# A transformer layer on one core: weight sums and norms in the passage into the feed-forward, and a rebuilt first stage

## The chip and the metric

The kernel runs on one core of a Trainium2 chip. Its engines are TensorE (PE, with its weight loads listed apart as PEld), VectorE (DVE), ScalarE (ACT), GpSimd (POOL), and SyncE (SP), which here issues nearly all DMAs. The metric is device time in microseconds (us). Of several runs the median is taken.

## What is computed

One layer over 1024 latent and 256 context tokens, model width 1024, all in f32:

```python
h = _modulate(_rmsnorm(x), sh_a, sc_a)          # for latent and context tokens
qa, ka, va, cq, ckv, krope = jnp.split(h @ w_in, SPLIT_POINTS, axis=-1)
# cq, ckv: own rmsnorm, then w_q_up, w_kv_up
oa = _map_query_blocks(lambda q1, q2: _diff_attend(q1, q2, k1, k2, va, lam), lq1, lq2)
ob = _map_query_blocks(lambda q: _softmax_attend(q, kb, vb), lqb)
new_lat = x_lat + g_a * _merge_heads(oa, ob, lam_init, diff_subln, w_out)
h = _modulate(_rmsnorm(new_lat), sh_f, sc_f)
new_lat = new_lat + g_f * _swiglu(h, w_ffn_in, w_ffn_out)
return _rmsnorm(new_lat, final_norm)
```

The shifts, scales and gates come from `silu(c) @ w_ada + b_ada`. `_rmsnorm` divides by the root of the mean square over the width.

## The kernel before

Activations lie transposed: 128 features on the partitions, tokens along the free axis, so that the width is eight chunks `k`. A product of full precision is made of a high and a low part (both fp32r): weights wh, wl and activations hH, hL, three products each. `split` makes the parts: ScalarE rounds to the high part, VectorE (or another engine, `lo_eng`) subtracts to get the low one.

The norm of a column of tokens needs a sum over partitions. `column_sums` multiplies tiles of 128 tokens with two columns of ones; `inverse_rms` takes root and reciprocal, and the result has tokens on the partitions. `spread` brings it back along the free axis: it scales the identity by each 128 of the values, which gives diagonals (`dg`), and multiplies them with ones on PE. `low_diag` and `low_norm` do so for the two low-rank inputs, `Attention.diagonal` and `Attention.spread` for the eight blocks of the differential heads, `stat` and `spread_stat` around the feed-forward and for the last norm.

In the first stage (`p1`, up to `st.close()`, line 604) the squares of x are added up, the norm is spread into `rstd`, and for each chunk `k` the modulation's shift and scale are computed (`load_ada`, `split_ada`, `ada_part`, `ada_row`, `ada_columns`), x is modulated into hH and hL (`modulate`), and `group` adds the chunk's part of seven products with the low-rank columns of w_in (`mixw`, `lows`). The modulation's weights are the moving operand, 256 columns of two halves at once, with four columns of c (`c4`) as the weights in PE. On PE, DVE, ACT and POOL the order of this stage is the order of the program; a DMA is issued when its tile comes free. The later products with w_in, w_q_up and w_kv_up follow, and PE's order is there written out with `run_tasks`.

Attention's order is made by a planner (`attention_graph`, `schedule`): each operation has an engine, an assumed length, dependencies and a priority. The output projection (`project`, `residual`) follows.

The feed-forward goes through hidden chunks of 128 in a scheme of seven products instead of eight. `Hidden.sums` forms sums of weight blocks, `odd` and `even` split them, `last` splits one block, `p1` to `p7` are the products, 12 matmuls each. The first two chunks are done in the passage (`with tc.manual_schedule(engines=ENGINES)`, line 1544), where the program's order holds on all four engines, beside the norm of the second 512 tokens (`stat(512, 512, ...)`), its scaling (`scale2`, `shift2`) and the differences and splits of the tokens (`part`, `run`, `t3`, `t4`). The remaining chunks are a plain loop. Then w_ffn_out's products and the last norm (`final`) follow.

## Time and profile before

| | |
|---|---|
| three runs | 1570.89, 1575.68, 1576.01 us, median 1575.68 |
| profiled execution | 1571.2 us, span 1569.3, mean granted clock 0.985 |
| PE busy | 1499.1 us, 96% of the span |
| DVE, ACT, POOL busy | 1123.8, 752.5, 787.0 us |
| chain that ended last | PE 70%, DVE 10%, DMA 6%, POOL 5% |

A profile row of a matmul gives the instruction, not the call: an f32 product is two of them, an fp32r product one. Times that stand beside each other on PE overlap, since matmuls are pipelined; from start to start is what one costs. Idle time of an engine stands in square brackets with what ended it. The granted clock is the share of full speed that the throttle gave TensorE: 1.00 is 2.4 GHz, 0.50 is 1.2 GHz.

### The profile page before, as it was taken

The page shows a single profiled execution, that of the slowest core. Times are in us where ns is not written, and L with a number is a line of the kernel's source. Part 1 is how long each engine was busy: PE and PEld are TensorE (multiplying, and loading weights), DVE is VectorE, ACT ScalarE, POOL GpSimd, SP SyncE. Part 2 cuts the span into 40 slices and gives each one's busy share as a digit, 9 for nine tenths or more (in the row PEclk, how much of TensorE's full clock was granted, in tenths as well). Part 3 has the DMA queues.
Part 4 walks back from the last instruction along what each step waited for, and adds up shares of the span by engine and source line. Part 5 has one row for each costly group of instructions (what it writes and reads, how often), then busy time and mean ns, then how long its engine had stood idle before and what let it go on. Part 6 is the DMA issues. An engine that isn't in the chain of part 4 may idle for free.

```text
span 1569.3 us, 20682 instructions
## 1 busy us (share of the span) xinstructions
PE 1499.1 (96%) x7323; PEld 1210.4 (77%) x7323; DVE 1123.8 (72%) x1630; ACT 752.5 (48%) x1184; POOL 787.0 (50%) x547
## 2 busy tenths in 40 slices
PE   4899999989999999999999989999999999999997
PEld 2577888866777878888878767888888888888876
DVE  5758565569999879999854697655555555899883
ACT  5443321157777766777753454333333333444451
POOL 2437245526777847756511565755544441484221
PEclk8899999999999999999999989999999999999999
DMA  8426988596344434533146302322222224975633
GB/s 262 140 80 215 318 293 241 179 272 164 91 104 110 121 108 128 121 115 98 58 117 186 128 27 81 121 81 81 81 81 81 81 81 136 358 271 180 208 101 108
DMA packets 153922, 227.69 MB, mean 145 GB/s; under 512 B 11215, under 2 KB 80859, under 8 KB 153819
## 3 DMA queue, kind: packets, MB, share of 16 engines
q1 hardware_dynamic: 153547, 226.11, 46.7%
q8 instruction: 58, 0.95, 0.2%
q14 instruction: 45, 0.37, 0.1%
q10 hardware_dynamic: 272, 0.26, 0.0%
HBM read 172.53 MB, written 53.81 MB: 144 GB/s over the span
## 4 chain that ended last, share of the span: by engine, by line
PE 70%; DVE 10%; DMA 6%; POOL 5%; issue 3%; ACT 3%; SPq 1%; DVEq 0%; ACTq 0%; POOLq 0%
PE mm L1427 25%; PE mm L1715 10%; PE S L1056 10%; PE T L1118 6%; PE acc L1135 4%; PE acc L1140 3%; PE mm L1355 3%; PE mm L410 2%; PE ps L1355 1%; DMA wa<-in_w_ada_dram 1%; PE mm L600 1%; POOL sh L645 1%; POOL macc L681 1%; PE S L1355 1%; POOL e L1104 1%
## 5 line engine op out<-in xcount | busy, mean ns | idle before, releaser
L1056 PE MATMUL S<-kt,qt 128*128 128x512 f32 (+1 forms) x768 | 197.9, 362 | 10.5 <-ACT e L1090 8.7
L1090 ACT ACTIVATE e<-S,nm 128x1280 f32<-128x1280 f32 x128 | 170.3, 1331 | 46.4 <-DVE nm L1076 37.9
L1715 PE MATMUL mm<-block 128*128 128x512 f32 x792 | 179.7, 389 | 0.0
L1122 ACT ACTIVATE ph<-T 128x512 fp32r<-128x512 f32 x240 | 140.3, 597 | 81.9 <-PE T L1118 77.7
L1715 PEld LDWEIGHTS mm<-block 128*128 128x128 f32 x792 | 148.7, 188 | 30.8
L1072 DVE TENSOR_REDUCE nm<-S 128x1 f32<-128x1024 f32 x128 | 156.2, 1220 | 22.5 <-PE S L1056 21.1
L1126 DVE TENSOR_TENSOR pl<-T,ph 128x512 fp32r<-128x512 f32 x240 | 160.0, 682 | 15.8 <-ACT ph L1122 15.0
L1056 PEld LDWEIGHTS S<-kt,qt 128*128 128x128 f32 x768 | 131.8, 189 | 39.1 <-ACT e L1090 15.1
L1118 PE MATMUL T<-ident,e 128*128 128x128 f32 x960 | 140.4, 274 | 3.1 <-DVE pl L1126 1.7
L1110 POOL TENSOR_SCALAR e<-e,ls 128x1280 f32<-128x1280 f32 x64 | 88.0, 1376 | 102.6 <-DVE ls L1107 71.5
L1118 PEld LDWEIGHTS T<-ident,e 128*128 128x128 f32 x960 | 114.0, 141 | 32.1 <-DVE pl L1126 6.4
L1135 PE MATMUL acc<-ph,vt 128*128 128x512 f32 x320 | 120.9, 418 | 1.1 <-DVE otmp L1156 1.0
L1427 PE MATMUL mm<-fresh,wh 128*128 128x512 f32 x352 | 114.8, 406 | 3.4 <-DVE fresh L1580 3.3
L1427 PE MATMUL mm<-block,wh 128*128 128x512 f32 x352 | 112.2, 400 | 0.0
L1140 PE MATMUL acc<-pl,vt 128*128 128x512 f32 x240 | 104.6, 436 | 0.0
L1532 POOL TENSOR_TENSOR hd<-acc,v 128x512 f32<-128x512 f32 x22 | 29.7, 1349 | 149.4 <-DVE acc L1528 137.8
L344 ACT ACTIVATE wh<-wf 128x1024 fp32r<-128x1024 f32 (+1 forms) x51 | 52.2, 1025 | 103.4 <-issue 68.2
L1300 POOL TENSOR_TENSOR acc<-acc,sq 128x512 f32<-128x512 f32 x23 | 34.3, 1489 | 124.6 <-ACT sq L1298 124.0
L1104 POOL TENSOR_TENSOR e<-e,e 128x1280 f32<-128x1280 f32 x32 | 94.2, 2944 | 2.7
L410 PE MATMUL mm<-hH,wh 128*128 128x512 f32 (+1 forms) x256 | 95.2, 372 | 0.0
L410 PE MATMUL mm<-hH,wl 128*128 128x512 f32 (+1 forms) x256 | 94.0, 367 | 0.0
L410 PE MATMUL mm<-hL,wh 128*128 128x512 f32 (+1 forms) x256 | 93.8, 367 | 0.0
(357 smaller groups left out, 3613.3 us busy)
## 6 DMA issues: line engine op xcount, KB each, us to landing
wf<-in_w_ffn_in_dram SPq DMA_DIRECT2D x44, 512.0 KB, 3.7
hidD<-hd SPq DMA_DIRECT2D x44, 256.0 KB, 2.1
wh<-in_w_ffn_out_dram SPq DMA_DIRECT2D x21, 512.0 KB, 5.3
wl<-hidD SPq DMA_DIRECT2D x17, 512.0 KB, 5.7
wa<-in_w_ada_dram SPq DMA_DIRECT2D x16, 512.0 KB, 4.0
wa<-in_w_ada_dram SPq DMA_DIRECT2D x32, 256.0 KB, 3.7
qt<-QB SPq DMA_DIRECT2D x32, 256.0 KB, 4.7
qt<-QA SPq DMA_DIRECT2D x32, 256.0 KB, 4.9
```

What stands on the lines that cost most here:

```text
L410: PE.matmul(ps, a(k), b(k), start=start and i == 0, stop=stop and i == n - 1)
L1056: m = PE.matmul(S[:, c0:c0 + w], q, k[:, k0:k0 + w], start=s == 0, stop=s == len(job) - 1)
L1072: on_banks(DVE.tensor_reduce(self.stats(n)[0][:, i:i + 1], sl, AX.X, ALU.max, negate=True), BANKS[i], DVE)
L1090: m = ACT.activation(e, S[:, i * NT:(i + 1) * NT], AF.Exp, bias=self.s[n][0][:, i:i + 1], accum_out=total)
L1104: POOL.tensor_tensor(self.e[n, 0], self.e[n, 0], self.e[n, 1], ALU.add)
L1118: PE.transpose(self.T[c][:, b * P:(b + 1) * P], e[:, kc * P:(kc + 1) * P], ident)
L1122: ACT.activation(self.ph[c], self.T[c], AF.Copy)
L1126: DVE.tensor_tensor(self.pl[c], self.T[c], f32(self.ph[c]), ALU.subtract)
L1135: PE.matmul(self.acc[u, qh, j], vt[:, kc, v], self.ph[c], start=kc == 0 and i == 0, stop=False)
L1140: PE.matmul(self.acc[u, qh, j], self.kv[u][1][:, kc, v], self.pl[c], start=False, stop=kc == 9)
L1427: PE.matmul(ps, a[:, k, :], b, start=k == 0 and i == 0, stop=k == 3 and i == 2)
L1715: PE.matmul(ps[d], w[:, sl], x[:, t0:t0 + n], start=first and c == 0 and i == 0, stop=c == NH - 1 and i == 2, skip_group_check=not first)
```

## The change

It has five parts.

1. `spread` has no diagonals any more: the 128 values are the weights of an f32 product, repeated over 128 columns, and the identity is the moving operand; one product for each 128 tokens. All norms use it, and attention's planner loses the eight `diagonal` steps.
2. The host lays w_in and w_out out by chunks of 128 columns, and the modulation's first 2048 columns by chunk (`w_first`), so that a load is one run of 4 KB for each partition.
3. In the first stage the loads of x alternate with those of weights. Chunks 0 to 2 of the modulation use the f32 weights unsplit (`ada_whole`), chunk 0 before the norm's sums, chunk 1 behind its spread, chunk 2 in the loop's first pass. Chunks 3 to 7 are split two passes ahead, both subtractions on DVE, into a tile for each half, so that `ada_parts` has 32 products of 128 columns where `ada_part` had 16 of 256. The column turn (`ada_turn`) ends a pass.
4. In the passage, both first chunks' weight sums go to DVE; the first chunk's subtractions too; the second chunk's `even` goes to POOL.
5. In the passage, half of the first chunk's `p1` stands before the norm's sums and half behind them, and the second chunk's loads behind the spread.

```diff
-        d = op("Pool", 1.4, [root] + spreads[-1:], "diagonal", h, qh)
-        s = after("T", op("PE", 0.86, [d] + T[-2], "spread", h, qh, kind="diagonal"))
+        s = after("T", op("PE", 0.86, [root] + T[-2], "spread", h, qh, kind="diagonal"))
...
-    def spread(ps, rs, dg, n, eng):
+    def spread(ps, rs, n):
         for t in range(n // P):
-            eng.tensor_scalar(dg[:, t * P:(t + 1) * P], ident, rs[:, t:t + 1], 1.0, ALU.mult, ALU.mult)
-        PE.matmul(ps[:, :n], ones, dg[:, :n], start=True, stop=True)
+            PE.matmul(ps[:, t * P:(t + 1) * P], rs[:, t:t + 1].to_broadcast([P, P]), ident, start=True, stop=True)
...
-        return w_in.rearrange("(k p) c -> p k c", p=P)[:, :, c0:c0 + m]
+
+        return w_in[:, c0 * KD:(c0 + m) * KD].rearrange("p (k c) -> p k c", k=KD)
...
+    def load_x(k):
         dma(x[:, k, :], xT[k * P:(k + 1) * P, :])
-        if k == 1:
-            dma(smalls, vecs.rearrange("(c p) -> c p", p=P))
-            dma(lp, diff_lambda.rearrange("a b -> (a b)").partition_broadcast(P))
...
-            dma(was[i], w_ada.rearrange("(r p) c -> p r c", p=P)[:, :, i * D + k * P:i * D + (k + 1) * P])
+            dma(was[i].rearrange("p r c -> p (r c)"), w_first[k][:, i * D:(i + 1) * D])
...
+    def split_ada(wa, between=None):
+        wah, wal = ([part_tile(tag) for i in range(2)] for tag in ("wah", "wal"))
         for i in range(2):
-            ACT.activation(wah[:, i], wa[i], AF.Copy)
+            ACT.activation(wah[i], wa[i], AF.Copy)
         for i in range(2):
-            if i and between:
+            DVE.tensor_tensor(wal[i], wa[i], f32(wah[i]), ALU.subtract)
+            if i == 0 and between:
                 between()
-            (i and eng2 or eng).tensor_tensor(wal[:, i], wa[i], f32(wah[:, i]), ALU.subtract)
...
+    load_x(0)
+    load_x(1)
     was = [load_ada(0)]
-    mixw = [fetch_w(mix_cols(i), P) for i in range(2)]
+    dma(smalls, vecs.rearrange("(c p) -> c p", p=P))
+    dma(lp, diff_lambda.rearrange("a b -> (a b)").partition_broadcast(P))
+    mixw = []
+    for k in range(2, KD, 2):
+        load_x(k)
+        load_x(k + 1)
+        if k < KD - 2:
+            mixw.append(fetch_w(mix_cols(k // 2 - 1), P))
     was.append(load_ada(1))
     wkr = sp.tile([P, KD, 32], F32, name="wkr")
-    dma(wkr, win_cols(1920, 32))
-    was.append(load_ada(2))
...
-    def ada_part(w, i):
-        for r in range(KD):
-            PE.matmul(adp[0:4, 0:256], c4[:, r, :], w[i][:, :, r, :], start=r == 0 and i == 0, stop=r == KD - 1 and i == 1)
-
...
+    def ada_whole(k):
+
+        for i in range(2):
+            for r in range(KD):
+                PE.matmul(adp[0:2, i * P:(i + 1) * P], cv[:, r, :], was[k][i][:, r, :], start=r == 0, stop=r == KD - 1)
+
+    def ada_parts(w):
+
+        for i in range(2):
+            for n, p in enumerate(w):
+                for r in range(KD):
+                    PE.matmul(adp[0:4, i * P:(i + 1) * P], c4[:, r, :], p[i][:, r, :], start=r + n == 0, stop=r == KD - 1 and n == 1)
...
-    def modulate(k):
+    def scale(k):
...
+    def shift_low(k):
...
+        if k == 3:
+            ada_whole(0)
+        if k == 6:
+            row = ada_row(2)
+        if k in (5, 6):
+            split(*mixw[k - 5])
...
-    column_sums(msp, acc, NT)
-    adp = mm_tile()
-    wads = [ada_tiles()]
...
+    ada_turn(*row)
...
+    msp = mm_tile()
+    column_sums(msp, acc[0], 512)
+    column_sums(msp[:, 8:], acc[1], 768)
     inverse_rms(rsc, msp[:, 0:20], D)
-    ACT.activation(mixw[1][0], mixw[1][2], AF.Copy)
-    ada_part(wads[0], 0)
...
+    ada_columns(0)
     for i, (t0, n) in enumerate(SLICES):
         rb = mm_tile()
-        spread(rb, rsc[:, t0 // P:], dg[:, t0:t0 + n], n, POOL if i else DVE)
-        if i == 0:
-            DVE.tensor_tensor(wal[:, 1], was[0][1], f32(wah[:, 1]), ALU.subtract)
-            for w in mixw:
-                DVE.tensor_tensor(w[1], w[2], f32(w[0]), ALU.subtract)
+        spread(rb, rsc[:, t0 // P:], n)
         ACT.activation(rstd[:, t0:t0 + n], rb[:, :n], AF.Copy)
-    ada_part(wads[0], 1)
...
-    ada_columns(0, ada_row())
-    wads.append(split_ada(was[1], POOL, DVE, lambda: modulate(0)))
+    scale(0)
     mixw.append(fetch_w(mix_cols(2), P))
+    was.append(load_ada(2))
+    dma(wkr, win_cols(1920, 32))
+    ada_whole(1)
+    row = ada_row(2)
+    shift_low(0)
     split(*mixw[2])
-    wads.append(split_ada(was[2], POOL, DVE))
+    wads = {}
...
+    group(0, 0, low[:5])
+    ada_turn(*row)
     for k in range(KD):
-        if k == 0:
-            group(0, 0)
-        if k + 1 < KD:
-            for i in range(2):
-                ada_part(wads[k + 1], i)
-            row = ada_row()
         if k + 3 < KD:
             was.append(load_ada(k + 3))
-            wads.append(split_ada(was[k + 3], POOL, DVE if k % 2 else None))
-        if k == 3:
+        if k + 1 < KD:
+            ada_columns(k + 1)
+            scale(k + 1)
+        low_part = (lambda: shift_low(k + 1)) if k + 1 < KD else None
+        if k + 3 < KD:
+            wads[k + 3] = split_ada(was[k + 3], low_part)
+        elif low_part:
+            low_part()
+        if k == 4:
             split(wk2[:, :, 0:32], wk2[:, :, 32:64], wkr)
-        group(k, 1 if k == 0 else 0)
-        if k + 1 < KD:
-            ada_columns(k + 1, row)
-            modulate(k + 1)
         if k:
-            group(k, 1)
+            group(k, 0)
+        else:
+            group(0, 1, low[:5])
+            group(0, 0, low[5:])
+        if k + 2 < KD:
+            if k:
+                ada_parts(wads[k + 2])
+            else:
+                ada_whole(2)
+            row = ada_row(4 if k else 2)
+        group(k, 1, low if k else low[5:])
+        if k + 2 < KD:
+            ada_turn(*row)
...
-    def diag(dg, rs, n, eng):
-        for t in range(n // P):
-            eng.tensor_scalar(dg[:, t * P:(t + 1) * P], ident, rs[:, t:t + 1], 1.0, ALU.mult, ALU.mult)
...
-            PE.matmul(ps[:, :n], ones, dgs[min(bs[0], 1), i][:, :n], start=True, stop=True)
+            spread(ps, (rsq if bs[0] else rskv)[:, t0 // P:], n)
...
-                r = self.ms[:, h * 8 + qh * 4 + t:h * 8 + qh * 4 + t + 1]
-                POOL.tensor_scalar(self.dg[:, t * P:(t + 1) * P], ident, r, 1.0, ALU.mult, ALU.mult)
-
         def spread(self, h, qh):
             self.T["s"] = lps.tile([P, 512], F32, tag="T", name="T", bufs=2)
-            PE.matmul(self.T["s"], ones, self.dg, start=True, stop=True)
+            spread(self.T["s"], self.ms[:, h * 8 + qh * 4:h * 8 + qh * 4 + 4], 512)
...
-        return load_w(w_out.rearrange("(k p) c -> p k c", p=P)[:, :, d * P:(d + 1) * P], P)
+        return load_w(w_out[d], P)
...
-        dg = tmp_tile("dg", 1)[:, :n]
-        for t in range(n // P):
-            eng.tensor_scalar(dg[:, t * P:(t + 1) * P], ident, rs[:, t:t + 1], 1.0, ALU.mult, ALU.mult)
-        return dg
-
-    def spread_stat(dg, n):
+        return rs
+
+    def spread_stat(rs, n):
         rb = mm_tile()[:, :n]
-        PE.matmul(rb, ones, dg, start=True, stop=True)
+        spread(rb, rs, n)
...
+    def product(ps, w, name, ks=range(4)):
+
+        for k in ks:
             xh, xl = parts[(*name, k)]
             for i, (a, b) in enumerate(((w[0], xh), (w[0], xl), (w[1], xh))):
                 PE.matmul(ps, a[:, k, :], b, start=k == 0 and i == 0, stop=k == 3 and i == 2)
...
+        def sums(self, room=None, eng=POOL):
...
+            eng.tensor_tensor(s1[:, 0:4], u1, u2, ALU.add)
...
-                first[0].sums([oT[:, i].rearrange("p (k m) -> p k m", m=P) for i in range(2)])
+                first[0].sums([oT[:, i].rearrange("p (k m) -> p k m", m=P) for i in range(2)], DVE)
...
-        first[0].p1()
+
         first[0].last()
-        first[0].odd(POOL)
-        dg = stat(512, 512, DVE)
-        first[0].even(POOL)
+        first[0].odd()
+        first[0].a = mm_tile()
+        product(first[0].a, first[0].a11, (1, 1), range(2))
+        rs = stat(512, 512)
+        first[0].even()
+        product(first[0].a, first[0].a11, (1, 1), range(2, 4))
+        rb = spread_stat(rs, 512)
+        first[0].copy1()
+        first[0].p2(False)
         first[1] = Hidden(1, False)
         first[1].first(True)
-        first[0].p2(False)
-        rb = spread_stat(dg, 512)
-        first[1].sums()
         first[1].p1(False)
         first[1].p2(False)
...
-        first[1].odd(POOL)
+        first[1].sums(None, DVE)
+        first[1].odd()
         run(4, lambda k: (scale2(k + 4, 1, rb), shift2(k + 4, 1)),
             lambda k: DVE.tensor_tensor(nl[k, 0], nl[k + 4, 1], nl[k, 0], minus), *part(("T2",), lambda k: nl[k, 0]))
-        first[1].even()
...
+    def by_chunk(w):
+
+        return w.reshape(KD, P, -1).transpose(1, 0, 2).reshape(P, -1)
...
-        ("w_ada", a["w_ada"][0]),
+        ("w_first", a["w_ada"][0][:, :2 * D].reshape(KD, P, 2, KD, P).transpose(3, 1, 2, 0, 4).reshape(KD, P, 2 * D)),
+        ("w_ada", a["w_ada"][0][:, 2 * D:]),
...
-        ("w_in", a["w_in"][0]),
+        ("w_in", np.concatenate([by_chunk(a["w_in"][0][:, c:c + P]) for c in range(0, 1952, P)], axis=1)),
...
+        ("w_out", np.stack([by_chunk(a["w_out"][0][:, c:c + P]).reshape(P, KD, P) for c in range(0, D, P)])),
```

On PE, in the first stage, from the norm's sums (L416) to the first products of `group` (L600; after the change L620), the order before is

```order
L416 MATMUL mm<-ones,room 128x2 x10
L506 MATMUL mm<-wah,c_165 4x256 x8
L427 MATMUL mm<-room,ones 128x512 x2
L427 MATMUL mm<-room,ones 128x256
L506 MATMUL mm<-wal,c_165 4x256 x8
L515 MATMUL mm<-sel,row 128x2 x2
L600 MATMUL mm<-hH,wh 128x512
L600 MATMUL mm<-hH,wl 128x512
L600 MATMUL mm<-hH,wh 128x512
```

and with the change (L520 is `ada_whole`, L426 `spread`, L536 `ada_turn`)

```order
L536 MATMUL mm<-ident,row 128x2 x2
L416 MATMUL mm<-ones,wal 128x2 x10
L426 MATMUL mm<-ident,rsc 128x128 x10
L520 MATMUL mm<-wa,cT 2x128 x16
L620 MATMUL mm<-hH,wh 128x512
L620 MATMUL mm<-hH,wl 128x512
L620 MATMUL mm<-hH,wh 128x512
L620 MATMUL mm<-hH,wl 128x512
L620 MATMUL mm<-hH,wh 128x256
```

The diagonals' products are gone and the modulation of chunk 1 stands before the first group; that of chunk 0, with its turn, now stands ahead of the sums. A later pass has, between its two groups,

```order
L527 MATMUL mm<-wah,c_164 4x128 x8
L527 MATMUL mm<-wal,c_164 4x128 x8
L527 MATMUL mm<-wah,c_164 4x128 x8
L527 MATMUL mm<-wal,c_164 4x128 x8
L620 MATMUL mm<-hL,wh 128x512 x2
L620 MATMUL mm<-hL,wh 128x256
L620 MATMUL mm<-hL,wh 128x512 x4
L536 MATMUL mm<-sel,row 128x2 x2
```

where 16 products of 256 columns stood in two rows.

On DVE, in the passage, from the first hidden chunk's split to the scaling of the second 512 tokens (L1332; after the change L1337), the order before is

```order
L347 TENSOR_TENSOR wl<-wf,wh 128x1024
L1363 SCALAR_TENSOR_TENSOR block<-mm,modF,xr 128x512
L347 TENSOR_TENSOR ul<-wf,uh 128x512
L421 RECIPROCAL rs<-rs 128x4
L1316 TENSOR_SCALAR dg<-ident,rs 128x128 x4
L347 TENSOR_TENSOR wl<-wf,wh 128x512 x2
L1332 SCALAR_TENSOR_TENSOR block<-block,scF,mm 128x512 x2
```

and with the change (L1458 to L1461 are the sums)

```order
L347 TENSOR_TENSOR wl<-wf,wh 128x1024
L1458 TENSOR_TENSOR oT<-wf 128x512
L1459 TENSOR_TENSOR oT<-oT,wf 128x512
L1460 TENSOR_TENSOR oT<-wf 128x512
L1461 TENSOR_TENSOR oT<-wf,oT 128x512
L1368 SCALAR_TENSOR_TENSOR block<-mm,modF,xr 128x512
L347 TENSOR_TENSOR ul<-wf,uh 128x512
L347 TENSOR_TENSOR sl<-oT,sh 128x1024
L421 RECIPROCAL rs<-rs 128x4
L347 TENSOR_TENSOR wl<-oT,wh 128x1024
L347 TENSOR_TENSOR wl<-wf,wh 128x512 x2
L1337 SCALAR_TENSOR_TENSOR block<-block,scF,mm 128x512 x2
```

The diagonals (L1316) are gone; the four sums stand ahead of the last residual (L1368), and the subtractions of `odd` and `even` (sl and wl out of oT), which POOL did, stand around the reciprocal. In attention the orders of PE, DVE and ACT are the same before and after; POOL's lacks the eight diagonals.

## Rows read from the trace of the kernel before

**Rows 1.** Table of stages: us, busy us of each engine (instructions), granted clock, DMA share, GB/s.
```profile
0.00:108.40 108.40, 78.18 (x370) 52.87 (x371) 69.97 (x98) 52.62 (x79) 31.60 (x24) 0.92 0.53 160
108.40:300.00 191.60, 190.57 (x949) 156.45 (x948) 115.47 (x187) 59.84 (x107) 98.35 (x77) 0.98 0.79 255
...
560.00:800.00 240.00, 237.22 (x1388) 197.00 (x1387) 210.17 (x367) 172.78 (x281) 141.58 (x143) 1.00 0.39 104
...
890.00:950.00 60.00, 50.50 (x187) 35.95 (x186) 52.29 (x58) 32.27 (x51) 36.30 (x22) 0.89 0.14 42
```

**Rows 2.** Timeline of the first stage: start, us, engine, line, tiles, count [idle before <-releaser].
```profile
15.71 7.80 PE L560 MATMUL mm<-x,ones 128*128 128x512 f32 x12 [7.87 <-DMA x<-in_xT_dram]
...
23.35 2.29 PE L416 MATMUL mm<-ones,room 128*128 128x2 f32 x20
...
26.41 5.29 POOL L426 TENSOR_SCALAR room<-ident,rsc 128x128 f32<-128x128 f32 x6 [24.96 <-DVE rsc L421]
...
40.21 0.79 PE L600 MATMUL mm<-hH,wh 128*128 128x512 f32 x1 [4.07 <-ACT hH L525]
...
56.65 0.50 PE L600 MATMUL mm<-hH,wh 128*128 128x512 f32 x1 [0.65 <-ACT hH L525]
```

**Rows 3.** Table of two-microsecond stretches of the first stage, columns as in Rows 1.
```profile
16.00:18.00 2.00, 2.00 (x3) 0.88 (x3) 1.86 (x4) 1.84 (x4) 0.00 (x0) 1.00 1.04 403
...
22.00:24.00 2.00, 2.00 (x11) 1.21 (x9) 1.85 (x2) 1.66 (x2) 0.00 (x0) 1.00 1.16 290
...
28.00:30.00 2.00, 1.46 (x2) 0.00 (x0) 2.00 (x3) 0.50 (x1) 2.00 (x2) 0.50 0.82 167
```

**Rows 4.** Chain of waits (start, us, what), one late chunk; then one timeline row of PE.
```profile
96.54 1.87 PE mm L506 x16
98.41 3.03 PE mm L600 x14
101.44 0.53 PE mm L515 x4
101.97 1.70 PE mm L600 x7
...
49.52 1.90 PE L506 MATMUL mm<-wal,c 128*4 128x256 f32 x8
```

**Rows 5.** Timeline of VectorE in the first stage.
```profile
46.90 1.21 DVE L479 TENSOR_TENSOR wal<-wa,wah 128x1024 fp32r<-128x1024 f32 x1
...
64.80 1.81 DVE L524 SCALAR_TENSOR_TENSOR x<-x,modA,rstd 128x512 f32<-128x512 f32 x3
67.01 1.68 DVE L528 SCALAR_TENSOR_TENSOR hL<-x,modA,hH 128x1024 fp32r<-128x1024 f32 x2 [0.39 <-ACT hH L525]
```

**Rows 6.** Timeline of weight loads (PEld), f32, 512 columns; the page's group of transposes.
```profile
21.21 0.19 PEld L560 LDWEIGHTS mm<-x,ones 128*128 128x128 f32 x1 [0.24 <-issue]
21.64 0.19 PEld L560 LDWEIGHTS mm<-x,ones 128*128 128x128 f32 x1 [0.24 <-issue]
...
L1118 PE MATMUL T<-ident,e 128*128 128x128 f32 x960 | 140.4, 274 | 3.1 <-DVE pl L1126 1.7
```

**Rows 7.** Timeline of VectorE in the passage into the feed-forward.
```profile
890.36 0.75 DVE L1363 SCALAR_TENSOR_TENSOR block<-mm,modF,xr 128x512 f32<-128x512 f32 x1 [1.59 <-PE mm L1355]
894.32 0.69 DVE L347 TENSOR_TENSOR ul<-wf,uh 128x512 fp32r<-128x512 f32 x1 [3.21 <-ACT uh L344]
...
895.63 5.88 DVE L1316 TENSOR_SCALAR dg<-ident,rs 128x128 f32<-128x128 f32 x4
901.43 2.35 DVE L347 TENSOR_TENSOR wl<-wf,wh 128x512 fp32r<-128x512 f32 x2
903.71 1.39 DVE L1332 SCALAR_TENSOR_TENSOR block<-block,scF,mm 128x512 f32<-128x512 f32 x2
...
921.13 4.05 DVE L1580 TENSOR_TENSOR fresh<-block,fresh 128x512 fp32r<-128x512 f32 x3
```

**Rows 8.** Timeline of VectorE at the last norm.
```profile
1561.13 0.69 DVE L1316 TENSOR_SCALAR dg<-ident,rs 128x128 f32<-128x128 f32 x2
```

109 lines of the change are left out of this document (43 added, 66 removed).

## The prediction

> **What bounds the kernel now.** I read the table of stages first [rows 1]: how far TensorE (PE) is from being always busy in each stretch says what can be won there. From 108.4 to 300 us PE is busy 190.57 of 191.60 us, in the second half of attention 237.22 of 240.00, so nothing that shortens a wait can win more than 1.0 and 2.8 us there. Two stretches are loose: the first stage, 78.18 busy of 108.40, and the passage into the feed-forward, 50.50 of 60.00 and at a granted clock of 0.89. The change works on both.
>
> In the first stage the timeline [rows 2] shows one chain: the products that wait for x, the twenty two-column sums, then GpSimd (POOL) making six diagonals in 5.29 us, and only at 40.21 us the first product of the projection, after waiting 4.07 us for hH. The sums end at 25.64, so 14.6 us lie between them and that product. Chunk 1's first product comes at 56.65 [rows 2]. Later the chain of waits consists of PE work alone [rows 4]: 16 modulation products 1.87, 14 products 3.03, the turn of the row 0.53, 7 products 1.70, together 7.1 us a chunk. There the stage is PE-bound, and only a cheaper chunk would help.
>
> In the passage [rows 7] the norm's four diagonals take VectorE (DVE) 5.88 us, while POOL subtracts beside it; in the tail two take 0.69 [rows 8], so four would take 1.4. Behind them two halves of a weight take 2.35, and the scaling of the second half's tokens starts only at 903.71. From there on DVE is the slow engine: it is busy 52.29 of the stretch's 60.00 us [rows 1], and three subtractions take 4.05 beside POOL, where one alone takes 0.69 [rows 7].
>
> **The change, part by part.** *Loads of the first stage.* Ahead of the last pair of x pieces now stand 2.10 MB of weights (two pieces of 0.52 of the modulation, two of 0.52 of the projection). With x alone the queue moved 403 GB/s, with the 512-byte rows of the weights 290 [rows 3]. The new layout makes the weights 4 KB rows, whose speed no row shows: between these two, 5.2 to 7.2 us of transfer. I take 403, since x's 5 KB rows are the nearest. The sums move by less: the twelve products over x before them ran 7.80 us from 15.71 on, behind the data, so part of the delay is covered. Bounds 0 to 7.2 us; I take 3. The Trainium skill, page "DMA: Bandwidth & Descriptors", section "Specifications", gives 512 B as enough for line rate; by that rule the new layout would change no transfer, the delay would be 5.2 either way, and the 290 against 403 here speaks against it.
>
> *From the sums to the first product.* The sums end about 28.6. Square root and reciprocal stay, 0.6. The spreads become ten products of 128 columns against the identity. An f32 product is two instructions; at 512 columns these follow each other at 0.43 us at full clock [rows 6], so 0.107 at 128: 20 of them 2.1 us. Behind them PE does chunk 1's modulation in plain f32, 16 products, 32 instructions: 3.4. Both double at the low clock, and after the sums the clock did fall: 0.50 at 28 to 30 us [rows 3]. That is 6.1 to 11.6 us, while DVE scales chunk 0 beside it (1.81 [rows 5]); I take 8, between, as PE now has no wait of some us in it. First product at 36.6. Chunk 0 then costs 21 products (4.73 by [rows 4]), two turns (1.06) and chunk 2's modulation in f32 (3.4), with half a microsecond for a wait: chunk 1 begins at 46.3, against 56.65. The gain is 10 us, bounds 5 to 15.
>
> *Chunks 1 to 7.* The modulation products of chunks 3 to 7 go from 16 of 256 columns to 32 of 128, since each half now has a tile. No row shows an fp32r product of 128 columns. Below: the same columns at the same rate, 1.87 us [rows 4]. Above: the same 0.117 per instruction, 3.7. Still above stands the full f32 price, 6.8 (a rival, below). I take 2.8, half way. Chunks 1 to 5 cost 5.26 + 2.8 = 8.1 each, chunks 6 and 7 4.73 each: 46.3 + 40.3 + 9.5 = 96.1, against 108.4. DVE has 1.81 + 1.68 + 2 x 1.21 = 5.9 us a chunk and two short columns [rows 5], less than 8.1, now that POOL no longer subtracts beside it, and it works one chunk ahead. So the stage gives **-12 us**: 10 at its start, 2 in its later waits. With 1.87 it is -17, with 3.7 -8.
>
> *The passage.* The sums of the first hidden chunk go to DVE: 4 x 0.69 = 2.8 us, before the last residual, in front of which DVE idles 1.59 [rows 7]: that one comes up to 1.2 later, and the first half of PE's product covers it. Two subtractions of 1.21 go from POOL to DVE. The one ahead of the reciprocal falls into the 3.21 us in which DVE waited for ScalarE [rows 7]; the other adds 1.21. The diagonals' 5.88 go, and the weight's two halves, with POOL idle, cost 1.38 instead of 2.35. The spread, eight short instructions, is ready before DVE is. So the scaling starts at 903.71 - 5.88 + 1.21 - 0.97 = 898.1, 5.6 us sooner; the second half of PE's first product covers root and reciprocal. Behind it the second chunk's sums, 2.8 us, and a subtraction, 1.21, are added to DVE, and one subtraction of 1.21 goes to POOL: 2.8 us later. Against that, DVE is no longer slowed in the first half: of the kind of the three that took 4.05 instead of 2.1 there are sixteen, and each lost 0.66. POOL keeps the eight differences and gets the subtraction ahead of them, so it slows DVE later, not never. I count five to six of them as won, 3.7 us. Sum 5.6 - 2.8 + 3.7 = **-6.5 us**, bounds -2 (all of the contention comes back) and -9.5 (the 9.50 us that PE is idle [rows 1]).
>
> *All other norms.* Five spreads in the stage behind the first, eight in attention, two around the output projection, the rest in the last product: each was one f32 product of 512 columns, 0.86, and is four of 128 with the same columns, 0.86 if the weights load beside the products. The row for load and product of 128 columns together is the transposes: 140.4 us for 960, 0.146 each [rows 6], which would make eight instructions 1.17; so 0 to +0.3 each, 15 on a PE-bound path: 0 to +4.6. What goes: DVE's and POOL's diagonals. Where PE never waits [rows 1] that wins at most 1.0 + 2.8; in the tail the two diagonals are on the path, 0.69 [rows 8], at the last norm and hardly elsewhere. I take **-1 us**, bounds -4.5 and +4.6. In attention PE, DVE and ScalarE keep their order word for word; only POOL loses eight steps. The layouts of w_in and w_out change loads that PE does not wait for: 0.
>
> **Sum.** -12 - 6.5 - 1 = -19.5 against this execution's 1571.2 us (span 1569.3): 1551.7. The three runs shown have their median at 1575.68, 4.5 above the profiled execution; the next median may lie anywhere in that band, so I add 1 and say **1553**. Its own range, from the bounds above taken as partly independent, is 1541 to 1564.
>
> **Rivals.** *Short fp32r products cost the f32 price.* An f32 product of 128 columns is two instructions of 0.107; 32 of them 6.8 us a chunk instead of 2.8, five chunks +20: 1573, no change that can be told. For it: no row of this kernel has one, all fp32r products here have 256 columns or more. Against it: at 256 columns nothing is lost against 512 (16 x 256 columns in 1.87 us, 14 products in 3.03 [rows 4], both 2.2 columns per ns).
>
> *The modulation products run at the low clock.* Their weights are four columns wide, and eight of them took 1.90 us at 49.52 [rows 4] instead of 0.93, with 0.50 granted. If 6.8 us of them a chunk let the clock fall, they cost 13.6, five chunks +54, and the kernel takes 1607: slower. It decides from 8.3 us a chunk on, where five times the extra 5.5 reach 1580.4, the median and 0.3%. For it: that row, and the sums of [rows 2], after which the clock fell. Against it: from 62 us on 1.87 us of them a chunk kept full clock [rows 4].
>
> *Loads are not hidden behind 128 columns.* A weight load is listed at 0.19 us [rows 6]; eight in a row are 1.5 instead of 0.86, 15 spreads +10, and 1563. Against it stand the transposes' 0.146. The Trainium skill, page "TensorE: Matmul & The Clock Gate", section "Back-to-back issue gap", gives 81 ns for a load and product of 128 columns and 131 for 512; by that rule four short ones would be 2.5 times one long one, +1.3 a spread and 1572. Its 131 is not this kernel's: 14 products in 3.03 us are over 200 ns each.
>
> *The first stage's gain is given back.* The next stage starts with loads that wait for the stage's memory, and POOL's products. If its own chain of loads decides, 12 us are lost: 1565. Against it: PE is busy 190.57 of 191.60 there.
>
> **How the numbers follow.** A difference under 0.3% (4.7 us) can't be told from none. Forecast 0.66; short loads not hidden 0.07 and gain given back 0.05, both still faster; full f32 price 0.14, the same; low clock 0.08, slower. Faster 0.78, same 0.14, slower 0.08. The range must reach to the f32 price's 1573 above, and below to a stage with 1.87 and a passage of -9.5: 1538 to 1573.
>
> **What would show it.** First product of the projection near 37 us, chunk 1 near 46, the last before 100. A chunk's 32 modulation products in 2 to 4 us at granted clock 1.00; 6.8 would make the forecast wrong, as would 0.50. No wait of PE for a reciprocal or diagonal of more than 1 us in the passage, DVE's scaling about 5 us nearer to the last residual, POOL's subtraction behind it. Each spread's eight instructions in 0.9 to 1.2 us. Attention's and the later products' lengths the same within 2 us.

## The result, and the profile after

The changed kernel takes 1558.8 us (median of four executions, 1552.5 to 1560.8), the kernel before 1575.85 beside it (median of four, 1570.9 to 1579.6): a ratio of 0.9887, 95% interval 0.9853 to 0.992. The prediction was 1553, with a range of 1538 to 1573. The profiled execution after the change took 1558.29 us with a span of 1556.4; against the one before, of 1571.2 and 1569.3, that is 12.9 less, where the prediction's terms made 19.5.

The table of stages of the changed kernel; each stretch is shifted to the same place of the program as its counterpart in [rows 1], and the last two have the same lengths as there:

```profile
0.00:97.23 97.23, 81.40 (x512) 62.44 (x513) 59.04 (x98) 47.15 (x74) 0.89 (x8) 0.95 0.54 186
97.23:288.83 191.60, 188.56 (x967) 157.14 (x966) 112.54 (x173) 58.81 (x105) 99.48 (x80) 0.98 0.78 254
881.50:941.50 60.00, 52.05 (x209) 38.47 (x208) 51.74 (x66) 33.57 (x52) 23.70 (x15) 0.94 0.18 53
```

The first stage lost 11.2 us of length while PE's busy time rose from 78.18 to 81.40. In the passage PE is busy 52.05 of 60.00 instead of 50.50, at a granted clock of 0.94 instead of 0.89. POOL's 31.60 us in the first stage are 0.89.

The first stage in the timeline of PE, the counterpart of [rows 2]:

```profile
26.87 2.39 PE L416 MATMUL mm<-ones,wal 128*128 128x2 f32 x20
29.88 3.99 PE L426 MATMUL mm<-ident,rsc 128*128 128x128 f32 x20 [0.61 <-DVE rsc L421]
33.79 3.65 PE L520 MATMUL mm<-wa,cT 128*2 128x128 f32 x32
37.38 0.51 PE L620 MATMUL mm<-hH,wh 128*128 128x512 f32 x1
...
49.32 0.60 PE L536 MATMUL mm<-ident,row 2*128 2x2 f32 x4 [2.62 <-ACT row L531]
49.85 0.61 PE L620 MATMUL mm<-hH,wh 128*128 128x512 f32 x1
```

No wait for POOL or for hH stands ahead of the first product any more: sums, spreads and chunk 1's modulation follow each other with one wait of 0.61 us, and the projection begins at 37.38 instead of 40.21. The first fifteen of the twenty spread instructions run at the low clock, and chunk 1's modulation has 1.00 from 33.8 us on. Chunk 1 begins at 49.85 instead of 56.65, after a new wait of 2.62 us for ScalarE (ACT) and its copy of the row. The costliest of PE's waits behind the sums in the kernel before was (us in all, times, longest)

```profile
PE mm L600 <- ACT hH L525: 8.4, 5, 4.1
```

In all PE waited 15.1 us there, from the sums to the stage's end; in the changed kernel the 0.61 and the 2.62 are all.

A late chunk in the chain of waits, the counterpart of [rows 4] (start, us, what):

```profile
58.73 3.22 PE mm L620 x14
61.94 1.91 PE mm L527 x32
63.85 1.57 PE mm L620 x7
65.43 0.53 PE mm L536 x4
```

The 32 products of 128 columns (L527) take 1.91 us, within 0.04 of the 16 of 256 columns before. A chunk takes 7.23, all of it PE work, where the PE work of one was 7.13 before.

The table of four-microsecond stretches around the norm's sums, as [rows 3]:

```profile
16.00:20.00 4.00, 1.66 (x10) 0.97 (x9) 3.51 (x7) 3.55 (x6) 0.00 (x0) 0.92 1.02 418
20.00:24.00 4.00, 4.00 (x7) 1.53 (x6) 3.69 (x6) 3.61 (x6) 0.00 (x0) 0.65 1.01 409
24.00:28.00 4.00, 4.00 (x20) 2.41 (x19) 3.48 (x4) 2.01 (x3) 0.00 (x0) 1.00 1.01 375
28.00:32.00 4.00, 3.39 (x22) 3.30 (x22) 0.42 (x3) 0.29 (x2) 0.00 (x0) 0.70 0.40 156
```

The weights' 4 KB rows and x move together at 418 and 409 GB/s. The granted clock is 0.70 in the last of these stretches and 0.50 from 30 to 33 us, so the spreads took 3.99 us and not 2.1.

The timeline of VectorE (DVE) in the passage, the counterpart of [rows 7]:

```profile
882.75 0.74 DVE L1368 SCALAR_TENSOR_TENSOR block<-mm,modF,xr 128x512 f32<-128x512 f32 x1
...
889.52 1.40 DVE L1337 SCALAR_TENSOR_TENSOR block<-block,scF,mm 128x512 f32<-128x512 f32 x2
...
909.15 1.28 DVE L1504 TENSOR_TENSOR y<-acc,mm 128x512 f32<-128x512 f32 x2
912.54 0.78 DVE L347 TENSOR_TENSOR ul<-wf,uh 128x512 fp32r<-128x512 f32 x1 [2.12 <-ACT uh L344]
913.25 6.87 DVE L1588 TENSOR_TENSOR fresh<-block,fresh 128x512 fp32r<-128x512 f32 x4
920.04 1.27 DVE L1516 TENSOR_TENSOR acc<-acc,mm 128x512 f32<-128x512 f32 x2
921.23 4.08 DVE L1588 TENSOR_TENSOR block<-block 128x512 fp32r<-128x512 f32 x3
```

The same work of VectorE in the kernel before, further on than [rows 7] goes:

```profile
927.32 1.27 DVE L1499 TENSOR_TENSOR y<-acc,mm 128x512 f32<-128x512 f32 x2
...
930.41 2.49 DVE L1580 TENSOR_TENSOR fresh<-block,fresh 128x512 fp32r<-128x512 f32 x4
932.82 1.27 DVE L1511 TENSOR_TENSOR acc<-acc,mm 128x512 f32<-128x512 f32 x2
```

The timeline of POOL in the changed kernel:

```profile
909.12 2.40 POOL L347 TENSOR_TENSOR wl<-s,wh 128x1024 fp32r<-128x1024 f32 x1 [29.90 <-ACT wh L344]
911.48 4.70 POOL L1605 TENSOR_TENSOR block<-block 128x512 f32<-128x512 f32 x3
...
917.83 5.23 POOL L1607 TENSOR_TENSOR block<-block 128x512 f32<-128x512 f32 x3
```

The scaling of the second half's tokens begins 6.8 us behind the last residual (889.52 after 882.75), where it was 13.35 (903.71 after 890.36). DVE then runs up to 909.15 without POOL beside it. From there on POOL works without a gap, and beside it four subtractions take 6.87 us (2.49 before) and three take 4.08.

PE's waits in the passage, sums over 60 us (us, times, longest), in the kernel before:

```profile
PE mm L1321 <- DVE dg L1316: 3.8, 1, 3.8
PE mm L1427 <- DVE fresh L1580: 3.5, 3, 2.0
```

The same in the changed kernel:

```profile
PE mm L1432 <- DVE fresh L1588: 3.6, 5, 0.7
PE mm L1432 <- ACT fresh L1584: 1.5, 1, 1.5
PE mm L1432 <- ACT block L1584: 1.2, 1, 1.2
```

The 3.8 us of waiting for the diagonals are gone; waits for `fresh` and `block` further on have grown. All of PE's waits in these 60 us are 8.0, where they were 9.2.

### The profile page after: what moved, and what is told of

Read it like the earlier page. It is cut to its first block, busy times and chain, and to the rows that moved or that the text cites. A ratio compares the mean times of both kernels' runs of the same rounds, so it can differ in the third digit from the quotient of the medians.

```text
span 1556.4 us, 21067 instructions
## 1 busy us (share of the span) xinstructions
PE 1501.8 (96%) x7565; PEld 1228.7 (79%) x7565; DVE 1099.7 (71%) x1606; ACT 746.5 (48%) x1178; POOL 730.2 (47%) x489
## 4 chain that ended last, share of the span: by engine, by line
PE 79%; DVE 6%; DMA 6%; issue 3%; POOL 3%; ACT 2%; SPq 0%; DVEq 0%; ACTq 0%; POOLq 0%
PE mm L1432 26%; PE mm L1724 11%; PE S L1070 10%; PE mm L410 7%; PE T L1132 6%; PE acc L1149 4%; PE acc L1154 3%; PE mm L620 3%; PE mm L1360 3%; PE ps L1360 1%; PE S L1360 1%; POOL e L1118 1%; DMA wa<-in_w_ada_dram 1%; DVE nm L1086 1%; ACT e L1104 1%
## 5 line engine op out<-in xcount | busy, mean ns | idle before, releaser
L1124 POOL TENSOR_SCALAR e<-e,ls 128x1280 f32<-128x1280 f32 x64 | 87.9, 1374 | 128.4 <-DVE ls L1121 76.2
L1432 PE MATMUL mm<-block,wh 128*128 128x512 f32 x352 | 111.7, 398 | 0.0
```

Of the source, the lines that this page charges most:

```text
L1432: PE.matmul(ps, a[:, k, :], b, start=k == 0 and i == 0, stop=k == 3 and i == 2)
```

## The experiments

Every trace was cut at the same five places of the program: the first two-column sums behind the projection, the first score product, the end of the last product into `acc`, the end of the last out-projection product with a weight, the end of the feed-forward's products. The lengths between them, in us, worked out from the timelines, with the median of all executions and its ratio to the kernel before in the same set:

| kernel | first | behind it | attention | out | passage, feed-forward | rest | median | ratio, 95% interval |
|---|---|---|---|---|---|---|---|---|
| before | 111.7 | 210.5 | 480.2 | 87.8 | 449.6 | 229.4 | 1575.9 | |
| before_again | 111.7 | 209.9 | 480.7 | 87.8 | 447.7 | 228.0 | 1573.0 | 0.9995, 0.9984 to 1.0007 |
| changed | 100.6 | 210.4 | 483.0 | 87.9 | 445.7 | 228.9 | 1558.8 | 0.9887, 0.9853 to 0.992 |
| after_again | 101.0 | 210.5 | 480.5 | 88.0 | 446.0 | 231.6 | 1559.2 | 0.9914, 0.9892 to 0.9935 |
| first_only | 100.7 | 209.0 | 480.8 | 89.4 | 450.0 | 228.1 | 1559.9 | 0.9910, 0.9892 to 0.9927 |
| old_passage | 100.6 | 211.0 | 480.6 | 88.2 | 448.5 | 231.1 | 1560.1 | 0.9914, 0.9897 to 0.9932 |
| norm_diags | 100.4 | 209.5 | 479.5 | 89.4 | 447.4 | 226.3 | 1556.7 | 0.9892, 0.9874 to 0.9911 |
| first_diag | 102.6 | 211.4 | 480.6 | 88.0 | 447.4 | 229.4 | 1560.3 | 0.9911, 0.9898 to 0.9925 |
| rows512 | 103.2 | 213.4 | 481.6 | 88.2 | 447.4 | 230.2 | 1565.3 | 0.9940, 0.9923 to 0.9958 |
| row_ahead | 100.9 | 214.7 | 479.9 | 89.6 | 447.6 | 229.6 | 1560.1 | 0.9909, 0.9890 to 0.9929 |
| diffs_dve | 100.6 | 209.9 | 481.6 | 88.2 | 444.3 | 230.9 | 1558.7 | 0.9897, 0.9880 to 0.9915 |
| best_spread | 100.3 | 211.2 | 481.0 | 88.0 | 444.5 | 228.5 | 1555.3 | 0.9872, 0.9853 to 0.9891 |
| best_diags | 100.9 | 209.5 | 480.0 | 89.4 | 445.2 | 230.2 | 1548.8 | 0.9846, 0.9825 to 0.9868 |
| best_diags_again | 100.4 | 209.4 | 480.5 | 89.6 | 445.2 | 230.0 | 1552.4 | 0.9881, 0.9865 to 0.9898 |

In the column of the passage and the feed-forward, the plain loop over the remaining chunks takes 389.3 us in every trace, so its differences are the passage's. The three traces with the passage as before (before, before_again, first_only) have 447.7 to 450.0 (mean 449.1), the six with the changed one (changed, after_again, norm_diags, first_diag, rows512, row_ahead) 445.7 to 447.6 (mean 446.9). The passage's part of the gain is thus 2.2 us, and the first two traces, 3.9 apart, show it too large.

**The changed kernel once more (after_again).** No edit.

> The changed kernel once more, for a second trace of it. Attention took 482.0 us in its first trace (first score product 310.9, last product into acc 792.9) against 479.1 before, with the granted clock at 0.50 from 501.9 to 505 us, behind two-column sums. Theory: that fall comes and goes between executions and is no part of the change; a trace without it has attention at 479.5 to 480.5. Rival: the eight short spreads or GpSimd without its diagonals cost attention 2.9 us; then it is 481.5 to 482.5 again, with or without the fall. First stage (to the next sums) 100.6, last out-projection product to last product of the weights by the tokens 434.6, both within 1 us by either theory.

By the measure of that text attention is 479.4 us (311.5 to 790.9), the first stage ends at 101.02. The table of stretches at the same place of both traces:

```profile
500.00:502.00 2.00, 2.00 (x14) 2.00 (x14) 1.40 (x3) 0.60 (x1) 1.73 (x2) 0.66 0.00 0
502.00:504.00 2.00, 2.00 (x7) 1.51 (x6) 1.54 (x4) 0.87 (x1) 1.92 (x2) 0.50 0.00 0
```

```profile
500.00:502.00 2.00, 2.00 (x15) 1.82 (x16) 1.89 (x6) 0.60 (x1) 1.76 (x2) 1.00 0.00 0
502.00:504.00 2.00, 2.00 (x15) 1.74 (x14) 1.68 (x3) 1.76 (x3) 1.92 (x2) 1.00 0.00 0
```

In both, PE had waited about 1.15 us for an exponential and done the eight two-column sums; only in the first did the granted clock fall after it. The rows stand in this order, of the changed kernel's first trace and of its second. The theory holds: attention's 2.9 us are no part of the change.

**First stage alone (first_only).** All later hunks undone, but not the layouts:

```diff
-        rs = stat(512, 512)
+        dg = stat(512, 512, DVE)
...
-        first[1].sums(None, DVE)
-        first[1].odd()
+        first[1].odd(POOL)
```

> The kernel before with the new layouts and the new first stage alone; passage and all later norms as before. Theory: the first stage gives 11 us and keeps them, so 1560 to 1566 us against 1575, and the stage's end stands at 100.6 in the trace. Rival: a part is given back in the stage behind it or in attention; then the first score product stands later than 311.9, or the kernel is less than 8 us faster than before.

Measured 1559.9, with the stage's end at 100.74 and the first score product at 309.7: the gain is kept. It is also nearly the whole: this kernel and the changed one are within 1 us of each other (1559.9 and 1559.2 in the same set).

**The passage as before, without diagonals (old_passage).**

```diff
-        first[0].odd()
-        first[0].a = mm_tile()
-        product(first[0].a, first[0].a11, (1, 1), range(2))
+        first[0].odd(POOL)
...
-        first[1].sums(None, DVE)
-        first[1].odd()
+        first[1].odd(POOL)
```

> The changed kernel with the passage as before (the two chunks' sums on GpSimd, odd and even parts of the first on GpSimd and of the second on VectorE, the first product whole ahead of the norm's sums), but without the norm's diagonals. From the last out-projection product to the last product of the weights by the tokens it was 438.5 us before and 434.6 after the change. Theory: VectorE's freedom from GpSimd makes the gain, so without it the length is 436 to 438.5, the scaling of the second half's tokens starts 3 us or more later behind the last residual than in the changed kernel, and the kernel is 1.5 to 4 us slower than it. Rival: the diagonals' 5.88 us were the whole of it; then the length stays at 434 to 435.5.

By that text's measure the length is 437.4, and the scaling begins 11.8 us behind the last residual (892.25 after 880.42), 5.1 later than in the changed kernel. The theory's lengths fit: 448.5 against 445.7 and 446.0. But against all six traces of the changed passage that is 0.9 to 2.8 us more, 1.6 in the mean, and one of the three with the passage as before is shorter (447.7). That engines and order make more of the passage's gain than the diagonals is likely and not shown. In the median only 0.9 us are left, less than was expected and less than these sets can separate.

**The passage's differences on VectorE (diffs_dve).**

```diff
-        first[1].even(POOL)
+        first[1].even()
...
-            POOL.tensor_tensor(t4[k], nl[k, 0], nl[k + 4, 0], minus)
+            DVE.tensor_tensor(t4[k], nl[k, 0], nl[k + 4, 0], minus)
```

and the same for t3.

> The changed kernel with the second chunk's even part and all eight differences of the passage on VectorE, so that GpSimd does nothing beside it from 882 to 920 us. Theory: GpSimd's one block from 909.1 to 924.7 us slows VectorE (four subtractions in 6.87 us at 913.25, three in 4.08 at 921.23, where undisturbed ones take 0.62 each), some 8 us in all, and holds ScalarE 7.6 us; moved, the work costs VectorE 4.9 + 1.2 = 6.1. From the last out-projection product to the last product of the weights by the tokens 443.5 to 445 us against 445.7 and 446.0 (ends of products). Rival: VectorE is the slow engine and 6.1 us more on it is 2 to 6 us more of passage: 447.5 or longer.

Its VectorE timeline at the same work:

```profile
911.55 1.89 DVE L1605 TENSOR_TENSOR block<-block 128x512 f32<-128x512 f32 x3
...
916.36 2.50 DVE L1588 TENSOR_TENSOR fresh<-block,fresh 128x512 fp32r<-128x512 f32 x4
...
919.96 1.89 DVE L1588 TENSOR_TENSOR block<-block 128x512 fp32r<-128x512 f32 x3
```

and what POOL does beside it:

```profile
915.11 4.89 POOL L1458 TENSOR_TENSOR s<-wf 128x512 f32<-128x512 f32 x1 [37.48 <-DMA wf<-in_w_ffn_in_dram]
```

Four subtractions take 2.50 instead of 6.87 us and three take 1.89 instead of 4.08; the length is 444.3. The contention is what took the time, as the theory has it: eight differences cost VectorE 4.8 us and save it more than that. The four traces with this edit have 444.3 to 445.2, below all six without it. The two engines still meet, but now POOL's first sum of the third chunk takes 4.89 us instead of 1.73, and the loop behind is no longer for it (389.3). Why one engine is slowed here and the other there, no run shows. The Trainium skill, page "SBUF — State Buffer", section "Who interferes with whom", says that a VectorE operation on two SBUF inputs contends with GpSimd's reads of SBUF; these rows agree: 6.87 us beside POOL's differences, 2.50 without them. The median, 1558.7, does not show the 1.5 us.

**Diagonals again in the other norms (norm_diags).** `stat` and `low_norm` make diagonals on VectorE, attention on GpSimd:

```diff
-            spread(ps, (rsq if bs[0] else rskv)[:, t0 // P:], n)
+            PE.matmul(ps[:, :n], ones, dgs[min(bs[0], 1), i][:, :n], start=True, stop=True)
```

> The changed kernel with diagonals again in all norms but the first stage's and the passage's: on VectorE in the stage behind the first, the out-projection and the last products, on GpSimd in attention. Theory: these spreads decide nothing, 0 to 2 us in all: from the first stage's end to the first score product 210.3 (changed) or 210.6 (before), behind the last product over the hidden chunks 49.8 or 50.3, and attention at 479 to 482 as the clock has it. Rival: the short spreads cost attention 2.9 us and the kernel becomes 2 to 3 us faster than the changed one.

1556.7 against 1559.2: 2.4 us faster, as the rival had it, though the intervals overlap, and attention, 479.5, is only 1.0 shorter than in after_again. The spreads themselves cost nothing on PE, as two of them in the changed kernel show:

```profile
120.68 1.05 PE L426 MATMUL mm<-ident,rskv 128*128 128x128 f32 x8
121.58 1.06 PE L426 MATMUL mm<-ident,rsq 128*128 128x128 f32 x8
122.39 0.48 PE L410 MATMUL mm<-hH,wh 128*128 128x512 f32 x1
```

Eight short instructions every 0.90 and 0.81 us are the price of the one long product, 0.86. In the table the six traces with diagonals have 209.0 to 210.5 behind the first stage (mean 209.6), the six with spreads in which the clock fell no further time there 209.9 to 211.4 (210.7). In attention the spreads' traces are some 0.5 longer (leaving out the first, with its fall of the clock), in the out-projection 0.6 shorter, in the rest 1.3 longer (230.0 against 228.7, most of it the wait described at the end). That is some 2 us in all, as in the medians, and not clear of noise; what makes it stays open.

**Diagonals again in the first stage (first_diag).**

```diff
-        spread(rb, rsc[:, t0 // P:], n)
+        dg = (acc[0], acc[1][:, 0:512], acc[1][:, 512:768])[i]
+        for t in range(n // P):
+            (POOL if i else DVE).tensor_scalar(dg[:, t * P:(t + 1) * P], ident, rsc[:, t0 // P + t:t0 // P + t + 1], 1.0,
+                                               ALU.mult, ALU.mult)
+        PE.matmul(rb[:, :n], ones, dg, start=True, stop=True)
```

> The changed kernel with diagonals again in the first stage's norm alone: VectorE makes four, GpSimd six, and three f32 products of ones replace the ten short ones. Theory: the missing diagonals are a part of the first stage's gain; six on GpSimd took 5.29 us, chunk 1's modulation (3.65 us at full clock) covers some of it, so the projection's first product comes 2 to 5 us later than 37.38 and the stage ends at 102.5 to 105.5 instead of 100.6. Rival: chunk 1's modulation products cover the diagonals whole, then both stay within 1 us.

The first product comes at 39.52, the stage ends at 102.63, 2.0 us later: the theory's lower end. GpSimd's six took 2.23 us here, not 5.29; here VectorE makes diagonals beside them, there it subtracted. So the diagonals, made this way, are a fifth of the stage's gain.

**Rows of 512 bytes (rows512).**

```diff
-            dma(was[i].rearrange("p r c -> p (r c)"), w_first[k][:, i * D:(i + 1) * D])
+            dma(was[i], w_first.rearrange("(r p) c -> p r c", p=P)[:, :, i * D + k * P:i * D + (k + 1) * P])
```

and `win_cols` as before.

> The changed kernel with the modulation's and the projection's weights in the layout before (rows of 512 bytes instead of 4 KB); all orders as changed. Theory by the forecast: 2.10 MB of weights ahead of the last x pieces move at 290 instead of 403 GB/s or more, 2 us more, and each chunk's weights land later; the norm's sums start 1 to 3 us after 26.87 and the stage ends 1 to 3 us later, at 101.6 to 103.6. Rival: 512-byte rows move as fast (the Trainium skill, page "DMA: Bandwidth & Descriptors", section "Specifications", calls 512 B enough for line rate); then nothing moves by more than 0.5 us.

```profile
16.00:20.00 4.00, 1.50 (x11) 0.94 (x10) 3.23 (x6) 2.91 (x6) 0.00 (x0) 0.96 1.06 371
20.00:24.00 4.00, 4.00 (x6) 1.40 (x7) 3.52 (x5) 3.07 (x5) 0.00 (x0) 0.61 1.04 383
24.00:28.00 4.00, 3.72 (x15) 1.86 (x13) 3.71 (x5) 2.94 (x5) 0.00 (x0) 1.00 1.16 292
```

371, 383 and 292 GB/s, of x and weights together, stand where 418, 409 and 375 were, so here the long rows are faster, against the rule of the Trainium skill, page "DMA: Bandwidth & Descriptors", section "Specifications". But the sums came only 0.7 us later (27.60), less than the 1 to 3 expected; the first product is 2.1 later, since spreads and modulation met the low clock for longer (4.64 and 4.40 us instead of 3.99 and 3.65). The stage ends 2.6 later, and the kernel is some 6 us slower than the changed one (1565.3; 1558.8 and 1559.2 in other sets). In the trace 3 of them lie in the stage behind, where the granted clock fell once more (0.50 from 210.8 to 214.2) and PE waited 1.6 us more. The forecast put w_in's layout there at nothing; whether these 3 us are the layout's was not separated. The diagonals' 2.0 and the rows' 2.6 leave more than half of the first stage's 11.2 us; it lies in the rest of the rebuilding (order, chunks 0 to 2 unsplit, subtractions on one engine), which no run takes apart.

**The row's copy ahead (row_ahead).** In the first pass, chunk 2's row ahead of the second copy of chunk 3's weights:

```diff
         for i in range(2):
+            if i and later:
+                later()
+                ACT.activation(wah[i], wa[i], AF.Copy)
             DVE.tensor_tensor(wal[i], wa[i], f32(wah[i]), ALU.subtract)
```

> The changed kernel with one ScalarE copy moved: in the first chunk's pass the copy of chunk 2's modulation row goes ahead of the copy that waits for the second half of chunk 3's weights (issued at 44.32, landed 47.93, then ScalarE at 47.95, the row at 48.91, PE's turn at 49.32 after 2.62 us of waiting). Theory: chunk 1's first product was forecast at 46.3 and came at 49.85 because of this one queue; with the row ahead it comes at 47.0 to 47.5, the first stage ends 2 to 3 us sooner, at 97.6 to 98.6, and the kernel gains as much. Rival: VectorE or the landing of the weights holds the chunk anyway; then chunk 1 starts after 49 and the stage ends at 100 or later.

PE's turn came at 47.71, 1.6 sooner, without the wait; theory and rival both had chunk 1's start wrong. The stage ends at 100.86 all the same, as the rival had it. VectorE's timeline in this kernel:

```profile
59.12 0.34 DVE L543 TENSOR_SCALAR modA<-mm,bT 128x2 f32<-128x2 f32 x2
...
63.05 1.23 DVE L485 TENSOR_TENSOR wal<-wa,wah 128x1024 fp32r<-128x1024 f32 x1 [1.74 <-ACT wah L480]
...
66.92 0.34 DVE L543 TENSOR_SCALAR modA<-mm,bT 128x2 f32<-128x2 f32 x2
```

and PE's next turn in it:

```profile
64.28 0.60 PE L539 MATMUL mm<-sel,row 4*128 4x2 f32 x4 [0.49 <-ACT row L534]
```

From one `modA` to the next are 7.80 us, 1.74 of them a wait for ACT: VectorE waits for hH and the copies, ACT waits for the scaled x. That is more than PE's 7.23, so a start won earlier is lost a piece at each chunk: the turns are 1.6, 1.6, 1.1 and 0.5 us ahead of the changed kernel's, then 0.3 behind. In the changed kernel VectorE's round is 7.80 too, but PE's later start hides it: PE waits no more behind 49.85.

**Copies first, and the rest together (best_spread, best_diags, best_diags_again, before_again).** ACT's two copies of the weights ahead of hH from the second pass on, with the edits of row_ahead and diffs_dve; best_diags adds norm_diags' edit.

```diff
+        if k and k + 3 < KD:
+            for i in range(2):
+                ACT.activation(wah[i], was[k + 3][i], AF.Copy)
         if k + 1 < KD:
             ada_columns(k + 1)
             scale(k + 1)
```

> The changed kernel with two things: in the first stage the row's copy ahead of the split (as before) and, from the second pass on, ScalarE's two copies of a chunk's weights ahead of its three for hH, so that VectorE subtracts while ScalarE makes hH; in the passage the differences and the even part on VectorE. Theory: moving the row alone won nothing since VectorE and ScalarE take turns, 7.80 us a chunk in that trace with 1.74 us of VectorE waiting, more than PE's 7.23; without that wait they need about 6.3, PE sets the pace, and the stage ends 2 to 3 us sooner, at 97.5 to 98.8. The passage as in the run with the differences on VectorE, 444.3. In all 3 to 5 us under the changed kernel's 1559. Rival: the loads of a chunk's weights come too late for copies that stand first (three buffers, two a chunk); then chunks wait for DMA and the stage ends at 100 or later.

The stage ends at 100.25, and loads come too late, as the rival had it; ACT's timeline shows it:

```profile
52.08 1.06 ACT L634 ACTIVATE wah<-wa 128x1024 fp32r<-128x1024 f32 x1 [2.74 <-DMA wa<-in_w_first_dram]
...
58.72 1.06 ACT L634 ACTIVATE wah<-wa 128x1024 fp32r<-128x1024 f32 x1 [1.52 <-DMA wa<-in_w_first_dram]
```

The copies wait 2.74 and 1.52 us for their weights; PE's turn at 56.30 waits 1.74 behind the first, and behind that the granted clock is 0.72 and 0.85 (56 to 60 and 60 to 64 us). The tile of these weights has three buffers for two pieces a chunk; whether a fourth would bring the loads in time was not tried.

> The same with diagonals again in all norms but the first stage's and the passage's, as in the run with these. Theory: that run's median was 2.4 us under the changed kernel's; if the diagonals made that, this one is 1.5 to 3 us under the kernel of the run beside it. Rival: it was the chain of loads in the last products, which is 2 to 3 us longer in some executions of either form; then the two are within 1 us.

> The last kernel once more: its trace was of its slowest execution (1557.5 us, the others 1546 to 1550), and it decides whether diagonals in the later norms are worth anything. Theory: they are, by 2 us or more, as the two pairs of runs had it (1556.7 against 1559.2, 1548.8 against 1555.3): the median is again 1546 to 1551, and a trace at that time is shorter in the stage behind the first or in attention than 210.4 and 480.5. Rival: the pair differed by the falls of the clock alone; then the median is 1553 or more.

best_diags had 1548.8 beside best_spread's 1555.3, and 1552.4 the second time, between theory and rival; its traces have 209.5 and 209.4 behind the first stage and 480.0 and 480.5 in attention. It is the quickest kernel run: its ratios, 0.9846 and 0.9881, lie under the changed kernel's 0.9887 and 0.9914. Their intervals overlap, so its lead of some 0.4% is likely and not certain.

> The kernel before once more, for a second trace of it: its first trace was of an execution of 1571.2 us, and its medians were 1573.95 to 1575.85. Theory: the 3 to 5 us lie in the stages behind the first, as falls of the granted clock and longer waits for loads that come and go (as attention's 1.7 us and the last products' 2 to 3 us did between traces of the changed kernel), and the first stage ends at 111.7 again, within 0.5. Rival: the first stage itself is longer in a usual execution; then it ends at 114 or later, and what the change gives there is 14, not 11.

The first stage ends at 111.69, so what the change gives there is 11 in both traces. This trace too is of one of the shorter executions: 1567.7 us at a mean granted clock of 0.985, where the twelve had 1567.7 to 1575.7 at 0.978 to 0.986, and the changed kernel's four 0.989 to 0.991. By an estimate for a PE that is always busy, a clock of 0.982 instead of 0.985 costs 0.003 x 1570 = 4.7 us. The usual execution of before is some 5 us longer than each of the two traced ones (1575.85 against 1571.2, 1572.95 against 1567.7), and the medians differ by 15 to 17 us where the traces differ by 8 to 13. In which stages that lies no trace here shows.

## Why the prediction was right

**First stage: -12 forecast, -11.2 and -10.7 measured.** The load ahead of x at 403 GB/s was 418 and 409; the sums end at 29.3 instead of 28.6; from there to the first product 8 were forecast and 8.1 came. The 8, taken between bounds for the two clocks, became spreads mostly at the low clock (3.99) and chunk 1's modulation at full clock (3.65). Behind that two steps were off and cancelled, which is luck. "With half a microsecond for a wait" chunk 1 was to begin at 46.3; it came at 49.85, because ACT's copy of the row stood behind a copy that waited for a load: the queue was not followed. And the 32 short products were put half way between the bounds, 2.8 us; they cost 1.91, the lower one, so a chunk took 7.23 and not 8.1, five times 0.9 less. The last product ends near 96.9, forecast 96.1. "10 at its start, 2 in its later waits" became 6.8 (chunk 1 at 49.85 instead of 56.65) and 4.4. The reading behind it, "there the stage is PE-bound", rested on one late chunk: PE waited 5.3 us from chunk 1 on before, and nothing after the change. What the sum had not seen is that VectorE and ACT in turns need 7.80, so that 5.9 us of VectorE work were not the measure.

**Passage: -6.5 forecast, -3.9 between the first traces, -2.2 between the means of six and three.** The step that put the scaling "5.6 us sooner" held: 5.7 against the last out-projection product's end. At the two operations into y (909.15 after 881.8, the last out-projection product's end; 927.32 after 890.3 before) VectorE is 9.7 us ahead, more than forecast. The step that failed is "I count five to six of them as won, 3.7 us". At the next two into acc (920.04; 932.82) the lead is 4.3: four subtractions at 6.87 us instead of 2.49, and a wait of 2.12 instead of 1.22 for ACT, gave 5.3 back. Nor did "each" of the sixteen lose 0.66: before, seven of them took 1.32 to 1.77 us and nine ran undisturbed. After the change all sixteen run undisturbed, and the four behind them, which did so before, take 1.7 to 1.8 each. diffs_dve shows the cause by taking POOL's differences away. The bound -2, "all of the contention comes back", is close to what came.

**All other norms: -1 forecast, some +2 by norm_diags and the table, not clear of noise.** At the last norm the gain is there: PE waits 0.55 us for the reciprocal, where it waited 1.28 for diagonals (the first row is of the kernel before, the second of the changed one).

```profile
1561.88 1.13 PE L1321 MATMUL mm<-dg,ones 128*128 128x256 f32 x4 [1.28 <-DVE dg L1316]
1549.14 1.16 PE L426 MATMUL mm<-ident,rs 128*128 128x128 f32 x8 [0.55 <-DVE rs L421]
```

But the stages together are some 2 us longer with spreads, inside the +4.6 of the bound and on the other side of the value taken. The price of a spread (0.86, against 0.86 to 1.17) was right; "what goes: diagonals" won nothing where PE is always busy.

**The sum.** -11.2 - 3.9 + 2.3 (attention +2.8, mostly the clock, -0.1 behind the first stage, +0.1 in the out-projection, -0.5 in the rest) = -12.8, against -19.5. The median stands 0.5 above the profiled execution, where 1 was added. So 1553 became 1558.8: right on side and in range. The forecast gain was too large by the passage's contention and the other norms, and in this trace by a clock fall. By the means of the table the passage's 2.2 and the other norms' 2 nearly cancel, which fits first_only's 1 us.

**The rivals.** Short fp32r products at the f32 price: 32 took 1.91 us, where half as many plain f32 products (chunk 1's 16) took 3.65; refuted. Modulation at the low clock: every stretch from 60 to 100 us has 1.00; refuted. Loads not hidden behind 128 columns: 0.81 and 0.90 a spread; refuted. By the figure that the Trainium skill, page "TensorE: Matmul & The Clock Gate", section "Back-to-back issue gap", gives for a load and product of 128 columns, 81 ns, 32 would be 2.6 us, an estimate; 1.91 are 60 ns each (of weights four columns wide), so that figure is no floor here. The first stage's gain given back: first_only keeps it; refuted.
